# The context stream of a mixture layer in smaller steps, and latent attention with the second mixture on the right side of SBUF

## The chip, the core and the metric

The kernel runs on one core of one Trainium2 chip, as one launch. The metric is the device time of that launch in microseconds (us), the median of several executions.

## What is computed

Two blocks run one after the other on 512 tokens of width 1024, in float32. The first has two layers (attention, then a mixture of 32 experts of which each token takes two); the second has two layers of three mixers and a feed-forward part, on the 512 "latent" tokens and beside them on 256 "context" tokens. The reference, cut:

```python
def first_block(...):
    for i in range(2):
        y = swa_sink_gqa(h, ...) if i == 0 else mla(h, ...)
        h = layer_norm(alpha * h + y, ln_g[i, 0], ln_b[i, 0])
        y = hier_moe(h, ...)               # 4 groups x 8 experts, top 2, hidden 512
        h = layer_norm(alpha * h + y, ln_g[i, 1], ln_b[i, 1])
def hier_moe(...):
    hid = silu(ragged_dot(xs, w_gate, sizes)) * ragged_dot(xs, w_up, sizes)
    ys = ragged_dot(hid, w_down, sizes) * weight
    return segment_sum(ys, tok_sorted)
def second_block(x, c, ctx, c_ctx, ...):
    for layer in range(2):
        u = modulate(rmsnorm(x, ...), sh1, sc1) @ w_in[layer]
        uc = modulate(rmsnorm(xc, ...), sh1c, sc1c) @ w_in[layer]
        # gated linear attention, short convolution, neighbourhood attention
        # (the latent tokens read the context's states, keys and values)
        x = x + g1 * (concatenate([gla_lat, sc_lat, na_lat]) @ w_out[layer])
        x = x + g2 * conv_ffn(modulate(rmsnorm(x, ...), sh2, sc2), ...)
        if layer == 0:                     # the same for the context
            xc = xc + g1c * (... @ w_out[layer]); xc = xc + g2c * conv_ffn(...)
    return rmsnorm(x, final_norm_g)
```

The context's path needs nothing of the first block, so it can run beside it.

## The kernel before, in words

`whole` runs the stages in this order: attention of layer 0; the first mixture (`moe(0)`); latent attention (`mla`); the second mixture (`moe(1)`); the two latent layers of the second block (`mixer`, `ffn`); the final norm. Beside each mixture runs a piece of the context's path, the "context stream": layer 0's context mixers beside the first, `then` (layer 0's context feed-forward and layer 1's context mixers) beside the second.

A mixture takes the 32 experts in 16 pairs p = 0..15. Per expert, 6.29 MB of weights (gate, up, down; 2 MB each) come on SP's DMA queue (line 863) into wide buffers `wx` (and some others: `we` early ones, `ws`, and granules `w`). Per pair, tokens are gathered to columns `xg`; TensorE makes gate and up (L806) into PSUM `sc`; ScalarE (L807) and VectorE (L808) make the hidden rows; TensorE turns them (L815), VectorE copies them out as `hT` (L817, once per pair, so its 16 records are a clock of the pairs); TensorE multiplies by the down weights (L825), ScalarE scales into `y` (L827), and POOL adds the rows into `acc` in HBM with an indirect DMA (L742). After each expert of a pair p > 1 the Python loop calls `fill(n)`, which lets the context stream emit until it has emitted n TensorE instructions. That is the order in which the program is written; a scheduler then orders each engine's instructions, with the context stream's DMAs at high priority, and the pools decide which tile takes whose place: a tile waits until all tiles whose place it takes have been released.

The context stream's matmuls (128x256, PSUM banks `a` and `b`) split every float32 operand in a high and a low part and add three products (L240, L241, L242); the weights' parts `wh` (ScalarE, L235) and `wl` (VectorE, L236) are made on the chip. Its weights come on POOL's queue (L187), its small tables on SP's (L181).

SBUF is used as two stacks, left and right. Before the change the main stages lie on the left and the context stream on the right; `mla_down` (the first part of latent attention), with its weights' parts, lies on the right where the first context piece was, and so do buffers of the second mixture's early weights. In the latent mixers, `xT`, `sp` and `lp` lie on the right, the split weights `wh`, `wl` on the left, where the second mixture was.

`combine` ends a mixture: per tile of 128 tokens, x (read back from `acc`, L979) gets a row sum (L997), mean (L305), squares (L306), centring and gain (L307), a Newton reciprocal root (L274 to L289) and the bias (L309). Before the change its scratch and the vectors `ln_g`, `ln_b` (0.5 MB each when spread over the partitions, L976) take wide buffers, and the two vectors are loaded behind the use of the last gate and up weights.

Of the kernel before, what the change touches and what calls it, by code (L numbers as in the profile page):

```python
# [129 lines left out]
class Net:  # L130
    def __init__(self, nc, tc, ins, ctx):
        self.nc, self.tc, self.ins = nc, tc, ins
        self.side, self.banks, self.size = "left", {}, 1024
        self.cst = {}
        self.load_consts(self.pool(ctx, "consts", 1), 0)
        self.ident = self.c("ident")
        self.hp = self.pool(ctx, "hp", 1)
        self.wp = self.pool(ctx, "wp", 3)
        self.dp = self.pool(ctx, "dp", 1, space=bass.MemoryType.DRAM)

    def beside(self):

        b = copy.copy(self)
        b.side, b.cst, b.size = "right", dict(self.cst), 512
        b.banks = {t: (a, 1) for a, ts in (("a", "mm sc tp ua"), ("b", "po ub dn")) for t in ts.split()}
        return b
# [31 lines left out]
    def dma(self, out, src):  # L178

        with self.tc.high_priority() if self.side == "right" else nullcontext():  # L180
            self.nc.sync.dma_start(out, src)  # L181

    def load(self, out, src):

        if self.side == "right":
# [30 lines left out]
    def psum(self, es, **banks):  # L216

        if self.side == "left":
            self.banks = {t: (t, n) for t, n in banks.items()}
        self.pp = self.pool(es, "pp", 2, space=PSUM)  # L220
# [275 lines left out]
    def mla(self, xt):  # L496

        with ExitStack() as es:
            self.psum(es)
            self.held = ExitStack()  # L500
            self.wides = self.pool(self.held, "wide", 4), 4
            cp = self.pool(es, "cT", 1, "right")
            self.load_consts(cp, 4)
            cT = [cp.tile([128, 5, 512], F32R, name=f"cT{a}") for a in "hl"]
            kr = cp.tile([128, 4, 32], F32, name="kr")
            with self.stage(whp=4, side="right"):
                self.mla_down(xt, cT, kr)
# [105 lines left out]
    def moe(self, i, lg, meanwhile):  # L613
# [9 lines left out]
        with ExitStack() as ep:  # L623
            self.psum(ep, **(dict(mm=1, tp=1) if i else {}))
            self.load_consts(self.php, 3)
            parts = self._moe(i, lg, meanwhile)
        return self.combine(es, *parts)

    def _moe(self, i, lg, meanwhile):
# [205 lines left out]
        def stream(shape):  # L835
# [6 lines left out]
            if n < gen or (i == 0 and 17 <= n < 24):  # L842
                return [self.pool(es, f"early{n}", 1, side="right").tile(shape, F32, name="we")], nullcontext if n >= gen else self.late if n >= first else self.hold[1]
            turn = (n - gen if i or n < 17 else n - gen - 7) + base
# [103 lines left out]
        for p in range(16):  # L948
# [10 lines left out]
            for j in range(2):  # L959
                at, weight = to[2 * p + j]  # L960
                add_rows(at, down(hT[:, :, 64 * j:64 * j + 64], ws[j][2], weight))
                if p > 1:
                    fill(70 if i == 0 else 72)
            if p == 1 or (p == 0 and i == 0):
# [3 lines left out]
            elif p % 4 == 3 and p < 15:  # L968
                to = targets_of(2 * p + 2, 2 * p + 10)
        loaded, added = self.after("SP"), self.after("Pool")  # L970
        finished(beside)
        xs, lnp = self.new_x(), self.wide([128, 2, 1024])
        with loaded():
            lnp = [lnp[:, a] for a in range(2)]
            for w, nm in zip(lnp, ("ln_g", "ln_b")):
                nc.sync.dma_start(w, bcast_rows(ins[nm][i, 1], 1024))  # L976
        for t, x in enumerate(xs):
            with added():
                nc.gpsimd.dma_start(x, self.acc[i][128 * t:128 * t + 128])  # L979
            added = self.after("Pool")  # L980
        return xs, lnp

# [3 lines left out]

    def combine(self, es, xs, lnp):

        nc, V = self.nc, self.nc.vector
        with es:  # L990
# [189 lines left out]
    def mixing(self, l, st, xs=None, src=None, dst=None):  # L1180
# [12 lines left out]
        with ExitStack() as e1:  # L1193
            self.sp = self.pool(e1, "sp", 2, side="right")
            self.load_columns(self.sp, l)
            if not lat:
                self.mixer_pools(e1, l, lat)
            with ExitStack() as e2:
                xp = self.pool(e2, "xTp", 1, side="right")
                self.lp = self.pool(e2, "lp", 2, side="right")  # L1200
                if lat:
# [538 lines left out]
    def ffn(self, l, st, xs=None, rows=None):  # L1740
# [12 lines left out]
        xp = self.pool(e1, "xTp", 1, side="right")  # L1753
        self.sp = self.pool(e1, "sp", 2, side="right")
        self.load_columns(self.sp, l)
        self.lp = self.pool(e1, "lp", 2, side="right")
        tiles = []
# [104 lines left out]
    def whole(self, out):  # L1862
# [23 lines left out]
        xs = list(self.moe(0, lg, lambda: b.mixing(0, 1, src=ins["ctx_2"][0], dst=xc)))  # L1886
        lg = self.mla(xs)
        xs = self.moe(1, lg, then)
        with ExitStack() as es:
            self.psum(es, mm=2, sc=2, tp=2, po=2)  # L1890
            self.banks.update(ua=("mm", 2), ub=("sc", 2), dn=("po", 2))
            for l in range(2):
                xs = finished(self.ffn(l, 0, self.mixer(l, 0, xs)))
            self.sp = self.pool(es, "sp", 2, side="right")
            lp = self.pool(es, "lp", 2, side="right")
            g = lp.tile([128, 1024], F32, name="fg", bufs=1)
# [28 lines left out]
```

## Time and profile before

| | us |
|---|---|
| median of 3 runs | 3430.08 |
| the runs | 3419.17, 3430.11, 3430.08 |
| the profiled execution, whole | 3424.68 |
| its span, first to last instruction | 3422.9 |
| TensorE busy in the span | 3139.3 (92%) |
| first mixture's last `y` (L827) | ends at 920.5 |
| second mixture's first and last `hT` copy | 1256.6 and 1953.4 |

All rows below are of the profiled execution, and their times are microseconds from the start of its span. A median of a few runs lies some us from one execution, here 5.4 us above it.

### The profile page before, as it was taken

How to read it: one execution, taken by the hardware profiler on the slowest of the kernel's cores; microseconds unless marked ns; L12 is line 12 of the kernel's file. 1: busy time of each engine (PE TensorE's matmuls, PEld its weight loads, DVE VectorE, ACT ScalarE, POOL GpSimd, SP SyncE). 2: the span in 40 equal slices, each digit the busy share in tenths (PEclk: the TensorE clock that was granted, in tenths of full speed). 3: DMA queues.
4: the chain of work that ended last, by engine and by line, in shares of the span. 5: the costliest groups of instructions: out<-in, count | busy, mean ns of one | idle time of the engine just before them, and what ended most of it. 6: DMA issues, size and time to landing. Idle time of an engine off the chain costs nothing. (4 is left out here: it accounts for less than half of the span.)

```text
span 3422.9 us, 46600 instructions
## 1 busy us (share of the span) xinstructions
PE 3139.3 (92%) x17508; PEld 2123.4 (62%) x17508; DVE 1655.5 (48%) x4015; ACT 1172.2 (34%) x2322; POOL 406.2 (12%) x538
## 2 busy tenths in 40 slices
PE   8997999999699969999889759999999999999998
PEld 5454445544286636666445257767888777678887
DVE  3454242223266645555423056565555556755555
ACT  3331222222255324333122044344342442543332
POOL 0000221212100013232121100130000000400000
PEclk9998999999899979999999979999999999999999
DMA  8779989999931469888898932223233232333331
GB/s 287 264 272 351 352 327 338 364 355 388 329 121 43 165 225 379 317 321 314 302 359 322 387 99 80 76 74 111 87 99 98 81 92 67 81 100 93 97 94 56
DMA packets 282686, 716.01 MB, mean 209 GB/s; under 512 B 34936, under 2 KB 164008, under 8 KB 234584
## 3 DMA queue, kind: packets, MB, share of 16 engines
q1 hardware_dynamic: 250008, 634.80, 51.4%
q0 software_dynamic: 32448, 78.18, 7.4%
q8 instruction: 140, 2.29, 0.3%
q14 instruction: 90, 0.74, 0.1%
HBM read 691.76 MB, written 37.87 MB: 213 GB/s over the span
## 5 line engine op out<-in xcount | busy, mean ns | idle before, releaser
L236 DVE TENSOR_TENSOR wl<-w,wh 128x1024 fp32r<-128x1024 f32 (+4 forms) x467 | 437.1, 950 | 276.9 <-ACT wh L235 271.9
L235 ACT CAST wh<-w 128x1024 fp32r<-128x1024 f32 (+4 forms) x467 | 377.5, 827 | 512.5 <-PE po L242 116.2
L806 PE MATMUL sc<-wx,xg 128*64 128x512 f32 x1416 | 473.0, 613 | 23.1 <-DMA wx<-in_moe_w_up 16.9
L240 PE MATMUL mm<-xTh,wh 128*128 128x512 f32 (+1 forms) x672 | 263.3, 392 | 11.6 <-ACT xTh L235 6.1
L806 PEld LDWEIGHTS sc<-wx,xg 128*64 128x64 f32 x1416 | 133.0, 139 | 222.4 <-issue 176.9
L242 PE MATMUL mm<-xTh,wl 128*128 128x512 f32 (+1 forms) x672 | 262.2, 390 | 0.9 <-DVE wl L236 0.9
L241 PE MATMUL mm<-xTl,wh 128*128 128x512 f32 (+1 forms) x672 | 260.0, 387 | 0.0
L808 DVE TENSOR_TENSOR hid<-hid,sc 64x512 f32<-64x512 f32 x64 | 43.8, 685 | 304.7 <-ACT hid L807 304.4
L825 PE MATMUL mm<-wx,hT 128*64 128x512 f32 x704 | 173.7, 625 | 10.5 <-DVE hT L817 5.5
L807 ACT ACTIVATE hid<-sc 64x512 f32<-64x512 f32 x64 | 37.8, 591 | 382.5 <-PE sc L806 382.3
L806 PE MATMUL sc<-w,xg 128*64 128x512 f32 x352 | 168.0, 610 | 0.0
L742 POOL DMA_INDIRECT acc<-y,to x64 | 106.9, 1671 | 462.9 <-ACT y L827 262.1
L240 PEld LDWEIGHTS mm<-xTh,wh 128*128 128x128 f32 x672 | 127.9, 190 | 43.0 <-ACT xTh L235 6.6
L241 PE MATMUL sc<-xTl,wh 128*128 128x512 f32 (+1 forms) x384 | 146.0, 380 | 0.0
L242 PEld LDWEIGHTS mm<-xTh,wl 128*128 128x128 f32 x672 | 127.8, 190 | 28.8 <-DVE wl L236 1.3
L240 PE MATMUL sc<-xTh,wh 128*128 128x512 f32 (+1 forms) x384 | 145.6, 379 | 0.0
L242 PE MATMUL sc<-xTh,wl 128*128 128x512 f32 (+1 forms) x384 | 145.1, 378 | 0.0
L241 PEld LDWEIGHTS mm<-xTl,wh 128*128 128x128 f32 x672 | 127.7, 190 | 26.9 <-issue 0.7
L240 PE MATMUL a<-xTh,wh 128*128 128x256 f32 (+2 forms) x472 | 139.6, 296 | 4.7 <-ACT rs L1449 0.9
L240 PE MATMUL po<-wh,gTh 128*128 128x512 f32 x352 | 137.9, 392 | 3.8 <-DVE t2k L1771 2.8
L241 PE MATMUL po<-wl,gTh 128*128 128x512 f32 x352 | 137.1, 390 | 0.0
L242 PE MATMUL po<-wh,gTl 128*128 128x512 f32 x352 | 136.3, 390 | 0.0
(518 smaller groups left out, 6702.7 us busy)
## 6 DMA issues: line engine op xcount, KB each, us to landing
wx<-in_moe_w_up SPq DMA_DIRECT2D x89, 1024.0 KB
wx<-in_moe_w_down SPq DMA_DIRECT2D x88, 1024.0 KB
wx<-in_moe_w_gate SPq DMA_DIRECT2D x88, 1024.0 KB
g<-in_w_ada SPq DMA_DIRECT2D x48, 1024.0 KB
w<-in_ffn_w_up SPq DMA_DIRECT2D x176, 256.0 KB
w<-in_moe_w_gate SPq DMA_DIRECT2D x60, 512.0 KB
w<-in_ffn_w_up POOLq DMA_DIRECT2D x88, 256.0 KB
w<-in_ffn_w_down SPq DMA_DIRECT2D x44, 512.0 KB
```

The lines of the kernel that those rows point to most:

```text
L235: self.nc.scalar.copy(hi, src)
L236: self.nc.vector.tensor_tensor(lo, src, hi.bitcast(F32), op=ALU.subtract)
L240: mm(ps, ah, bh, start=start, stop=False)
L241: mm(ps, ah, bl, start=False, stop=False)
L242: mm(ps, al, bh, start=False, stop=stop)
L742: nc.gpsimd.indirect_dma_start(out=acc, out_offset=bass.IndirectOffsetOnAxis(ap=ix, axis=0), in_=y, in_offset=None, bounds_check=1023, oob ...
L806: nc.tensor.matmul(ps[r], xg[:, k], w, start=k == 0, stop=k == 7)
L807: nc.scalar.activation(hid[own], ps[other], AF.Silu)
L808: V.tensor_tensor(hid[own], hid[own], ps[own], op=ALU.mult)
L825: nc.tensor.matmul(py[64 * h:64 * h + 64], hT[:, k], w[:, 512 * h:512 * h + 512], start=k == 0, stop=k == 3)
```

## The change

The tests `side == "right"` become fields of their own (`second` for the context stream, `far` for the other side). A copy `m` of the main program with the sides swapped runs latent attention and the second mixture on the right; the context stream of the second mixture goes to the left. The latent layers keep their sides, so their left tiles now take the place of the context stream and their right tiles that of the second mixture. `combine` runs after the mixture's own pools are closed, in two small pools of its own, and loads `ln_g` and `ln_b` itself. In the second mixture `fill(72)` becomes `fill(62)`; what the stream has not emitted after the 28 calls is written behind the last expert (`finished(beside)`), ahead of the read-back of `acc`.

```diff
     def beside(self):
         b = copy.copy(self)
-        b.side, b.cst, b.size = "right", dict(self.cst), 512
+        b.side, b.second, b.cst, b.size = "right", True, dict(self.cst), 512
...
-            cp = self.pool(es, "cT", 1, "right")
+            cp = self.pool(es, "cT", 1, self.far)
...
-            with self.stage(whp=4, side="right"):
+            with self.stage(whp=4, side=self.far):
                 self.mla_down(xt, cT, kr)
...
-            parts = self._moe(i, lg, meanwhile)
-        return self.combine(es, *parts)
+            xs = self._moe(i, lg, meanwhile)
+        es.close()
+        return self.combine(i, xs)
...
                 if p > 1:
-                    fill(70 if i == 0 else 72)
+                    fill(70 if i == 0 else 62)
...
-        loaded, added = self.after("SP"), self.after("Pool")
+        added = self.after("Pool")
         finished(beside)
-        xs, lnp = self.new_x(), self.wide([128, 2, 1024])
-        with loaded():
-            lnp = [lnp[:, a] for a in range(2)]
-            for w, nm in zip(lnp, ("ln_g", "ln_b")):
-                nc.sync.dma_start(w, bcast_rows(ins[nm][i, 1], 1024))
+        xs = self.new_x()
...
-    def combine(self, es, xs, lnp):
+    def combine(self, i, xs):
...
+        with ExitStack() as es:
+            cp = self.pool(es, "comb", 2)
+            self.sp = self.pool(es, "csp", 2)
+            lnp = cp.tile([128, 2, 1024], F32, name="lnp", bufs=1)
+            for a, nm in enumerate(("ln_g", "ln_b")):
+                nc.sync.dma_start(lnp[:, a], bcast_rows(self.ins[nm][i, 1], 1024))
...
-                both = self.wide([128, 2, 1024])
+                both = cp.tile([128, 2, 1024], F32, name="lntt")
...
         xs = list(self.moe(0, lg, lambda: b.mixing(0, 1, src=ins["ctx_2"][0], dst=xc)))
-        lg = self.mla(xs)
-        xs = self.moe(1, lg, then)
+        m = copy.copy(self)
+        m.side, m.far = "right", "left"
+        lg = m.mla(xs)
+        b.side = b.far = "left"
+        xs = m.moe(1, lg, then)
```

The names of `combine` have new line numbers in the changed kernel: L976 is L992, L997 is L1000, the mixture's L806 to L828 are one higher, and L1128, L1155 are L1131, L1158.

**Between the first mixture and latent attention, ScalarE.** `wh` are the parts of `mla_down`'s weights, `xTh` the high parts of its turned input (two per tile of 128 tokens), L997 or L1000, and L306, are `combine`'s. Before:

```order
L235 CAST wh_7561<-w_7559 128x768
L827 ACTIVATE y_7349<-mm_7340,wy_6901 128x512
...
L306 ACTIVATE wx_7377,ln_s_7381<-x_7368,ln_n_7380 128x1024
...
L306 ACTIVATE wx_7400,ln_s_7404<-x_7368,ln_n_7403 128x1024
L997 ACTIVATE wx_7446,sums_7447<-x_7368 128x1024
L235 CAST xTh_7498<-tp_7500 128x4x128
L235 CAST xTh_7498<-tp_7507 128x4x128
L306 ACTIVATE wx_7423,ln_s_7427<-x_7368,ln_n_7426 128x1024
L235 CAST xTh_7498<-tp_7514 128x4x128
L235 CAST xTh_7498<-tp_7521 128x4x128
L306 ACTIVATE wx_7446,ln_s_7450<-x_7368,ln_n_7449 128x1024
```

And in the changed kernel:

```order
L828 ACTIVATE y_7363<-mm_7354,wy_6901 128x512
L235 CAST wh_7569<-w_7567 128x768
...
L306 ACTIVATE lntt_7386,ln_s_7390<-x_7368,ln_n_7389 128x1024
L1000 ACTIVATE lntt_7409,sums_7410<-x_7368 128x1024
L235 CAST wh_7587<-w_7585 128x768
L1000 ACTIVATE lntt_7432,sums_7433<-x_7368 128x1024
L306 ACTIVATE lntt_7409,ln_s_7413<-x_7368,ln_n_7412 128x1024
L1000 ACTIVATE lntt_7455,sums_7456<-x_7368 128x1024
L306 ACTIVATE lntt_7432,ln_s_7436<-x_7368,ln_n_7435 128x1024
L306 ACTIVATE lntt_7455,ln_s_7459<-x_7368,ln_n_7458 128x1024
L235 CAST xTh_7506<-tp_7508 128x4x128
L235 CAST xTh_7506<-tp_7515 128x4x128
```

The first `xTh` moved behind the squares (L306) of all four tiles, where it stood behind those of two; on VectorE the low parts `xTl` moved behind L307 and L309 of all four tiles in the same way. The `wh` moved behind the last `y`.

**Between the second mixture and the latent layers, ScalarE.** Here `wh` are the parts of the latent layer's `w_in`, L1128 (L1131) scales a tile by its root. Before:

```order
L827 ACTIVATE y_17111<-mm_17102,wy_16117 128x512
L827 ACTIVATE y_17125<-mm_17116,wy_16117 128x512
L997 ACTIVATE wx_17157,sums_17158<-x_17130 128x1024
...
L235 CAST xTh_17153<-t2k_17235 128x4x128
L1155 ACTIVATE t2k_17272,ss_17274<-x_17130 128x512
L235 CAST xTh_17153<-t2k_17242 128x4x128
L235 CAST wh_17475<-w_17473 128x768
L235 CAST wh_17481<-w_17479 128x768
L235 CAST wh_17487<-w_17485 128x768
L235 CAST wh_17493<-w_17491 128x768
L1128 ACTIVATE t2k_17272<-x_17130,rs_y_17281 128x512
```

In the changed kernel:

```order
L808 ACTIVATE hid_17064<-sc_17065 64x512
L235 CAST wh_17491<-w_17489 128x768
L808 ACTIVATE hid_17064<-sc_17084 64x512
L828 ACTIVATE y_17119<-mm_17110,wy_16094 128x512
L235 CAST wh_17497<-w_17495 128x768
L828 ACTIVATE y_17133<-mm_17124,wy_16094 128x512
L235 CAST wh_17503<-w_17501 128x768
L235 CAST wh_17509<-w_17507 128x768
L1000 ACTIVATE lntt_17176,sums_17177<-x_17138 128x1024
...
L235 CAST xTh_17163<-t2k_17261 128x4x128
L1131 ACTIVATE t2k_17291<-x_17138,rs_y_17300 128x512
```

All four `wh` moved from behind the first tile's `xTh` to the mixture's last expert. VectorE's four `wl` moved with them.

**The same place, SP's queue.** `wx`, `ws` (`in_moe_w_down`) are the last expert's weights, `w<-in_w_in_2` the latent layer's. Before:

```order
L863 DMA ws_17054<-in_moe_w_down 128x2048
L189 DMA w_17479<-in_w_in_2 128x2x384
L189 DMA w_17485<-in_w_in_2 128x2x384
L976 DMA wx_17131<-in_ln_g 128x1024
L976 DMA wx_17131<-in_ln_b 128x1024
```

In the changed kernel:

```order
L864 DMA ws_17062<-in_moe_w_down 128x2048
L189 DMA w_17495<-in_w_in_2 128x2x384
...
L181 DMA pcol_17155<-cols_76 128x320
...
L189 DMA w_17637<-in_w_in_2 128x2x416
L189 DMA w_17643<-in_w_in_2 128x2x416
L189 DMA w_17649<-in_w_in_2 128x2x416
L992 DMA lnp_17173<-in_ln_g 128x1024
L992 DMA lnp_17173<-in_ln_b 128x1024
```

`ln_g` and `ln_b` moved behind five small tables and three more weights, each of which waits until VectorE has split the granule that it takes; their own place is free only when the last down matmul of the mixture has run.

In the second mixture the scheduler keeps the context's matmuls inside: ahead of the gate and up matmuls of pair 1 stood 54 of them and now stand 16, ahead of pair 2 214 and 137, ahead of pair 6 1176 and 1100, ahead of pair 7 1432 and 1369, ahead of pair 9 1611 and 1603, and all 1959 stand ahead of pair 14 in both kernels; none stands behind the last expert. On SP, of four loads of expert weights that stood behind some twenty small tables of the context (pair 8), three stand ahead of them now.

## Rows read from the trace of the kernel before

**Rows 1.** Part 1 of the page: busy time and share of the span, TensorE.

```profile
PE 3139.3 (92%) x17508; PEld 2123.4 (62%) x17508; DVE 1655.5 (48%) x4015; ACT 1172.2 (34%) x2322; POOL 406.2 (12%) x538
```

**Rows 2.** Windows: us, busy of PE PEld DVE ACT POOL, clock, DMA share, GB/s.

```profile
1300.00:1400.00 100.00, 100.00 (x607) 63.38 (x607) 47.78 (x95) 35.74 (x68) 32.11 (x39) 1.00 0.97 362
...
1600.00:1700.00 100.00, 91.65 (x579) 53.40 (x577) 46.24 (x106) 22.49 (x43) 17.66 (x18) 0.96 0.81 286
1700.00:1800.00 100.00, 86.47 (x405) 40.14 (x402) 26.46 (x63) 25.09 (x53) 22.28 (x25) 0.92 0.97 366
1800.00:1900.00 100.00, 93.49 (x568) 48.10 (x567) 32.54 (x83) 26.93 (x47) 12.66 (x13) 0.98 0.90 339
```

**Rows 3.** The second mixture's copies of `hT` (L817), one per pair.

```profile
L817 DVE COPY hT<-tp x16: 655/692/693, 1256.6 to 1953.4; 128x512 f32<-128x512 f32 x16
```

**Rows 4.** Timeline of VectorE: the copies of pairs 8 and 12.

```profile
1674.37 0.66 DVE L817 COPY hT<-tp 128x512 f32<-128x512 f32 x1
...
1857.61 0.69 DVE L817 COPY hT<-tp 128x512 f32<-128x512 f32 x1 [3.29 <-PE tp L815]
```

**Rows 5.** Timeline of TensorE in the second mixture: two context matmuls, one after the other.

```profile
1403.34 0.28 PE L240 MATMUL b<-xTh,wh 128*128 128x256 f32 x1
1403.46 0.28 PE L241 MATMUL b<-xTl,wh 128*128 128x256 f32 x1
```

**Rows 6.** Windows at pair 8 and at the second mixture's end.

```profile
1680.00:1700.00 20.00, 13.62 (x70) 4.90 (x69) 4.08 (x13) 1.91 (x3) 5.69 (x4) 0.89 0.79 266
...
1900.00:1960.00 60.00, 49.15 (x207) 17.50 (x205) 4.82 (x7) 5.60 (x9) 5.80 (x4) 0.97 1.01 409
1960.00:1980.00 20.00, 2.29 (x12) 0.55 (x8) 5.24 (x13) 7.08 (x13) 4.16 (x6) 0.63 0.57 179
1980.00:2000.00 20.00, 7.66 (x26) 6.86 (x27) 17.57 (x59) 13.25 (x28) 0.00 (x0) 0.51 0.40 144
```

**Rows 7.** Timeline of SP's queue at pair 8: issues of small tables and of weights.

```profile
1672.73 1.32 SPq L181 DMA_DIRECT2D mrow<-mod  x2
...
1685.51 0.35 SPq L181 DMA_DIRECT2D xc<-xctx  x1
1685.95 0.41 SPq L863 DMA_DIRECT2D wx<-in_moe_w_gate  x1
...
1687.61 0.67 SPq L863 DMA_DIRECT2D ws<-in_moe_w_up  x1
```

**Rows 8.** Timeline between the first mixture and latent attention.

```profile
919.84 0.69 ACT L827 ACTIVATE y<-mm,wy 128x512 f32<-128x512 f32 x1
...
934.29 0.15 DVE L305 TENSOR_SCALAR ln_n<-sums 128x1 f32<-128x1 f32 x1 [8.03 <-ACT wx L997]
...
938.43 0.15 DVE L305 TENSOR_SCALAR ln_n<-sums 128x1 f32<-128x1 f32 x1
...
938.66 1.94 PE L253 MATMUL tp<-cst,x 128*128 128x128 f32 x8 [19.18 <-DVE ln_n L305]
...
940.80 1.05 ACT L235 CAST xTh<-tp 128x512 fp32r<-128x512 f32 x2
...
972.32 0.90 PE L545 MATMUL tp<-cst,cn 128*128 128x128 f32 x3 [3.35 <-ACT cn L539]
```

**Rows 9.** Timeline between the second mixture and the latent layers.

```profile
1962.39 0.69 ACT L827 ACTIVATE y<-mm,wy 128x512 f32<-128x512 f32 x1 [3.80 <-PE mm L825]
...
1974.31 1.28 DVE L307 SCALAR_TENSOR_TENSOR wx<-x,ln_n,wx 128x1024 f32<-128x1024 f32 x1 [0.31 <-DVE ln_n L305]
...
1986.67 1.97 PE L1124 MATMUL tp<-cst,t2k 128*128 128x128 f32 x8 [24.38 <-ACT t2k L1128]
...
1992.31 2.31 ACT L235 CAST wh<-w 128x768 fp32r<-128x768 f32 x3
...
1993.20 0.69 PE L240 MATMUL mm<-wh,xTh 128*128 128x384 f32 x1 [4.56 <-ACT wh L235]
...
1998.94 0.72 ACT L1128 ACTIVATE t2k<-x,rs_y 128x512 f32<-128x512 f32 x1
```

More of the change, by code (lines that the diff above doesn't have):

```diff
@@ L132, in __init__ @@
         self.nc, self.tc, self.ins = nc, tc, ins
-        self.side, self.banks, self.size = "left", {}, 1024
+        self.side, self.far, self.second, self.banks, self.size = "left", "right", False, {}, 1024
         self.cst = {}
@@ L178, in dma @@
     def dma(self, out, src):
-        with self.tc.high_priority() if self.side == "right" else nullcontext():
+        with self.tc.high_priority() if self.second else nullcontext():
             self.nc.sync.dma_start(out, src)
     def load(self, out, src):
-        if self.side == "right":
+        if self.second:
             with self.tc.high_priority():
@@ L216, in psum @@
     def psum(self, es, **banks):
-        if self.side == "left":
+        if not self.second:
             self.banks = {t: (t, n) for t, n in banks.items()}
@@ L842, in stream @@
             if n < gen or (i == 0 and 17 <= n < 24):
-                return [self.pool(es, f"early{n}", 1, side="right").tile(shape, F32, name="we")], nullcontext if n >= gen else self.late if n >= first else self.hold[1]
+                return [self.pool(es, f"early{n}", 1, side=self.far).tile(shape, F32, name="we")], nullcontext if n >= gen else self.late if n >= first else self.hold[1]
             turn = (n - gen if i or n < 17 else n - gen - 7) + base
@@ L980, in _moe @@
             added = self.after("Pool")
-        return xs, lnp
+        return xs
     def wide(self, shape):
         return self.wides[0].tile(shape, F32, name="wx", tag="wx", bufs=self.wides[1])
-    def combine(self, es, xs, lnp):
-        nc, V = self.nc, self.nc.vector
-        with es:
+    def combine(self, i, xs):
+        nc = self.nc
+        with ExitStack() as es:
[4 more added lines that the diff above has]
+                nc.sync.dma_start(lnp[:, a], bcast_rows(self.ins[nm][i, 1], 1024))
+            lnp = [lnp[:, a] for a in range(2)]
             turn = nullcontext
             for t, x in enumerate(xs):
-                both = self.wide([128, 2, 1024])
+                both = cp.tile([128, 2, 1024], F32, name="lntt")
                 ta, tb = both[:, 0], both[:, 1]
@@ L1193, in mixing @@
         with ExitStack() as e1:
-            self.sp = self.pool(e1, "sp", 2, side="right")
+            self.sp = self.pool(e1, "sp", 2, side=self.far)
             self.load_columns(self.sp, l)
@@ L1198, in mixing @@
             with ExitStack() as e2:
-                xp = self.pool(e2, "xTp", 1, side="right")
-                self.lp = self.pool(e2, "lp", 2, side="right")
+                xp = self.pool(e2, "xTp", 1, side=self.far)
+                self.lp = self.pool(e2, "lp", 2, side=self.far)
                 if lat:
@@ L1752, in ffn @@
             xs = self.rows_in(es, rows)
-        xp = self.pool(e1, "xTp", 1, side="right")
-        self.sp = self.pool(e1, "sp", 2, side="right")
+        xp = self.pool(e1, "xTp", 1, side=self.far)
+        self.sp = self.pool(e1, "sp", 2, side=self.far)
         self.load_columns(self.sp, l)
-        self.lp = self.pool(e1, "lp", 2, side="right")
+        self.lp = self.pool(e1, "lp", 2, side=self.far)
         tiles = []
@@ L1893, in whole @@
                 xs = finished(self.ffn(l, 0, self.mixer(l, 0, xs)))
-            self.sp = self.pool(es, "sp", 2, side="right")
-            lp = self.pool(es, "lp", 2, side="right")
+            self.sp = self.pool(es, "sp", 2, side=self.far)
+            lp = self.pool(es, "lp", 2, side=self.far)
             g = lp.tile([128, 1024], F32, name="fg", bufs=1)
```

## The prediction

> **What bounds the kernel now.** The page comes first: TensorE is busy 92% of the span [rows 1], so on the whole the kernel goes at TensorE's pace, and only the places where it idles, or works at half clock, have much to give. The windows show where they are. In the second mixture TensorE is full at 1300 to 1400 us, and falls to 91.65, 86.47 and 93.49 us per 100 in the three windows from 1600, while the DMA share is 0.97 again from 1700 [rows 2]. The copies of `hT` time the pairs: 15 steps from 1256.6 to 1953.4 us [rows 3], with pair 8 at 1674.37 and pair 12 at 1857.61 [rows 4]. So the eight steps to pair 8 take 417.8 us, 52 each, and are TensorE's; the four to pair 12 take 183.2, 46 each, and are of both; the three to the last take 95.8, 31.9 each. These last are the DMA's: two experts are 12.58 MB, at the 409 GB/s of that window 30.8 us, with the engines' share at 1.01 [rows 6]. Behind the mixture TensorE then does 9.95 us of work in 40, at granted clocks of 0.63 and 0.51 [rows 6]. A smaller hole of the same kind lies at the first mixture's end: 19.18 us [rows 8]. The change touches these three places; everything after some 2040 us is the latent layers, whose order of instructions is the same in both kernels.
>
> **The change part by part.**
>
> *The context's smaller steps.* What moves is only the place of context matmuls among those of the experts. Counted from the two orders, 77 fewer stand ahead of pair 2, 76 ahead of pair 6, 63 ahead of pair 7, 8 ahead of pair 9, and none from pair 14 on. Two follow each other at 0.12 us [rows 5], so TensorE comes to a pair's gate and up matmuls up to 77 x 0.12 = 9.2 us earlier in the stretch that is TensorE's, and nothing of it is left in TensorE's own work by pair 9. The gain, if any, is what the DMA makes of it: wide buffers come free up to 9 us earlier, and the weights of later pairs are fetched earlier. It has idle share to use (0.81 in the window from 1600 [rows 2]). All of it kept would be 9 us; if the DMA gives it back where context work bunches at pairs 8 to 10, it is 0. I take 4, the middle, because the share is 0.97 from 1700 on, where a lead is spent on the one resource that has none over. The order has no context work behind the last expert, so the 31.9 us steps of the tail have no less to carry and no more.
>
> *SP's queue at pair 8.* Issues of small tables run from 1672.73 to 1685.51 us, and four loads of 1 MB follow behind them, the first at 1685.95 and the last at 1687.61 [rows 7]. In the 20 us after 1680 TensorE is busy 13.62 and the DMA share is 0.79 [rows 6]: the queue, not the bytes, was late there. Three of the four now stand ahead of the tables. The idle DMA time in that window is 0.21 x 20 = 4.2 us, which bounds the gain; but these loads also wait for buffers that the preceding pair's down matmuls hold, which a better place does not release. And the context's read-back now stands behind weights that wait, which may hold its next block. From 4 gained to 6 lost (TensorE's 6.38 us idle there, once more); I take 2 gained.
>
> *`combine` in its own pools, first mixture.* Squares and centring of all four tiles now come before the first `xTh` and `xTl`. A tile's period is 938.43 - 934.29 = 4.14 us [rows 8], so the last tile's squares lie 3 periods after the first's, at about 934.3 + 12.4 + 1.3 (the centring takes 1.28 [rows 9]) = 948 us, and `xTh` follows at some 948 to 949, against 940.80 [rows 8]. That is 8 us late. It is not all lost: before, the turned input of tiles 1 to 3 came one period after another, and TensorE's matmuls followed at that pace, with a wait of 3.35 us at 972.32 for the normalised rows [rows 8]; now all four tiles are there at once. I take 5 lost. The ends: nothing lost, if the later tiles catch up wholly; 10, if the low parts on VectorE come one more half period late. The vectors `ln_g`, `ln_b` are now loaded when the last down matmul has run, about 919.8 [rows 8]; the centring that needs them begins at 934.5 (behind the mean at 934.29), and each is a transfer of 0.5 MB. At the 179 GB/s of the other boundary [rows 6] the 1 MB takes 5.9 us; that is hidden under the read-back of `acc`, with some 9 us over.
>
> *`combine` and the sides, second mixture.* Four `wh` and their `wl` now lie on free space of the left and are made during the last expert. Before, the first matmul waited 4.56 us, ended by a `wh`, and went at 1993.20; `wh` x3 took 2.31 us from 1992.31, just ahead of it [rows 9]. Without them it is `xTh` that ends the wait, some 1 to 2 us sooner. The next tile's scaling, at 1998.94, stood behind the fourth `wh` and goes up to 2.7 us earlier, but its turning stands in TensorE's order behind 24 matmuls at half clock. From 5 gained to 0; 2 to 3 is where the `wh` row puts it.
>
> The late vectors work against it. They wait for the last down matmul, at about 1962.4 (the last `y` begins there), and stand behind three weight loads that wait for splits (three `wh` take 2.31 us [rows 9], and the `wl` follow them); so they reach the DMA at some 1966, and the centring wants them at 1974.31 [rows 9]. At the 179 GB/s of that window [rows 6] 1 MB takes 5.9 us: 1972, 2 us in hand, with the read-back of `acc` and the weights in the same engines. The cover is the read-back; if it is gone, the centring waits up to 3 us, and with it the whole chain to 1986.67. I take 0.5 lost, so 2 gained for the place.
>
> The sum: -4 - 2 + 5 - 2 = -3 us. Against the profiled execution, 3424.7, that is 3421.7. The median of the runs shown lies 5.4 us higher than that execution and the lowest run 5.5 below it; I give 3424, half way back to the median.
>
> **The clock, and a rule weighed.** With TensorE idle 24.38 us [rows 9] the granted clock is 0.63 and 0.51, near the lower of its two levels (1.2 of 2.4 GHz) [rows 6]; the 7.66 us of work from 1980 on would be about 4 at full clock. Nothing in the new order fills that hole.
>
> Where the change could hurt is the DMA behind pair 8. At 409 GB/s with the engines' share at 1.01 [rows 6] an expert load of 1 MB is worth 2.6 us. Three context matmuls (the high and low products) use one new weight block of 128x256 floats, 131 KB, or half of one where both token tiles share it; so the 55 matmuls that now bunch between pairs 7 and 9 stand for 9 to 18 blocks, 1.2 to 2.4 MB, 3 to 6 us of DMA time that the expert loads there wait for at most. The sum takes these bytes as moved, not added, and so at nothing. The Trainium skill, "DMA: Bandwidth & Descriptors", section "Queues, rings and completion order", says that each DMA engine takes turns between the queues that have work for it, packet by packet. By that rule a context load on POOL's queue takes half of every engine from the expert load that it meets, whatever SP's order is, and the moved bytes do hurt where the experts are short: the sum would be 0 to +3 instead of -3. No row before shows the two queues' rates apart in one such moment; the rule is the slower rival's second half below.
>
> **The rivals.**
>
> *Faster: the middle of the mixture opens.* From pair 8 to pair 12 the four steps take 183.2 us, while the DMA alone would need 4 x 30.8 = 123 for the experts. What is over, 60 us, is context weights, TensorE's context work and the two waiting on each other: TensorE idles 8.35 + 13.53 + 6.51 = 28.4 us in the three windows from 1600 [rows 2]. If the smaller steps and the new place of the loads let the two overlap, up to 20 of these 28 us come back. For it: DMA share 0.81 in the first of these windows, so bytes could have come earlier. Against it: 0.97 in the second, and context work that ends at the same pair. It would give 3421.7 - 18 = about 3404, at most 3400.
>
> *Slower: the chains at the boundaries grow and nothing comes back.* The place is the first mixture's end. If `xTl` as well as `xTh` waits for all of VectorE's four tiles, the first matmul goes at 952, and the late start passes on undiminished: 11 us; it decides against the change as soon as it exceeds 8, the gains of the other terms. With the gains of the steps at 0 too, the sum is +11 - 2 = +9, about 3434 from the profiled execution, and 3439 from the median. A full slowdown beyond 0.5% needs the bunched context work as well (55 matmuls more from pair 7 to pair 9 than before, 6.6 us of TensorE, and 3 to 6 us of DMA), just where both are short, so that buffers of the tail come free late: +7, and 3446 with the rest.
>
> *It doesn't do what it says.* The rest of the stream behind the mixture is none, by the order of the instructions; the step of 62 or 72 then decides only some 9 us of order, and what remains are the two boundaries: 5 - 2 = +3, 3428 from the profiled execution and 3433 from the median.
>
> **How the numbers follow.** My forecast of small terms that nearly cancel, with the rival in which nothing is done, both within half a per cent of 3430 (17 us, about what a measurement of this kernel can tell from no change): 0.36 and 0.2. The open middle: 0.27, and nearly all of it ends below 3413. The growing chains: 0.17, most of it ending above 3447 only if the bunching is added, which I give about two thirds. With some spill from each case: faster 0.27, same 0.58, slower 0.15. The range goes from 3402, the open middle nearly whole, to 3444, the grown chains from the median; the likeliest case's own is 3412 to 3435.
>
> **What would show it.** Steps: the copies of `hT` up to pair 7 some 5 to 9 us earlier relative to pair 0, and the last one 3 to 6. SP at pair 8: the DMA share above 0.9 in the 20 us where it was 0.79. First boundary: first `xTh` about 28 us behind the last `y` (21 before), and the wait before L545 shorter. Second: no wait for `wh`, first matmul 29 us behind the last `y` (30.8 before). Wrong would be: context matmuls in the hole behind the mixture, a wait of the centring for `ln_g`, or steps between pairs 8 and 12 that sum to under 165 us or over 190.

## The result, and the profile after

The changed kernel takes 3448.02 us in the median of 4 runs (3443.27 to 3449.49); the kernel before, run beside it, 3427.03 (3419.17 to 3430.11). The ratio is 1.0067, with a 95% interval from 1.0052 to 1.0083: some 23 us slower, outside the range that was given. The profiled execution of the changed kernel took 3443.27 us, 18.6 more than that of before.

TensorE runs the same 17508 matmuls and is busy 5.5 us longer (part 1 of the page of the profile; [rows 1] before):

```profile
PE 3144.8 (91%) x17508; PEld 2129.2 (62%) x17508; DVE 1657.9 (48%) x4015; ACT 1172.8 (34%) x2322; POOL 406.4 (12%) x538
```

So most of the loss is in waits; the longer busy time has to do with a stretch at half clock in the latent layers, which comes up below. The pairs of the second mixture, by the copies of `hT` ([rows 3] before), say in which stages the loss arises:

```profile
L818 DVE COPY hT<-tp x16: 682/691/692, 1265.5 to 1964.7; 128x512 f32<-128x512 f32 x16
```

Pair 0 comes 8.9 us later than before and pair 15 11.3 later, though the first mixture's last `y` (L828) comes 2.3 us earlier. Most of the loss is there ahead of the second mixture. The timeline of the first boundary ([rows 8] before) shows it:

```profile
917.59 0.69 ACT L828 ACTIVATE y<-mm,wy 128x512 f32<-128x512 f32 x1 [2.75 <-PE mm L826]
917.95 0.46 SPq L992 DMA_DIRECT2D lnp<-in_ln_g  x1
...
928.01 2.21 POOL L976 DMA_DIRECT2D x<-acc  x4 [5.29 <-issue]
...
931.95 1.06 ACT L1000 ACTIVATE lntt<-x 128x1024 f32<-128x1024 f32 x1 [2.79 <-issue]
...
933.13 0.15 DVE L305 TENSOR_SCALAR ln_n<-sums 128x1 f32<-128x1 f32 x1 [2.78 <-ACT lntt L1000]
...
934.47 1.04 ACT L1000 ACTIVATE lntt<-x 128x1024 f32<-128x1024 f32 x1
...
937.49 1.94 PE L253 MATMUL tp<-cst,x 128*128 128x128 f32 x8 [19.99 <-DVE ln_n L305]
...
942.58 1.06 ACT L1000 ACTIVATE lntt<-x 128x1024 f32<-128x1024 f32 x1 [2.87 <-issue]
...
947.57 0.15 DVE L305 TENSOR_SCALAR ln_n<-sums 128x1 f32<-128x1 f32 x1
...
950.55 1.28 DVE L309 SCALAR_TENSOR_TENSOR x<-lntt,rs_y,lnp 128x1024 f32<-128x1024 f32 x1
...
951.99 1.07 ACT L235 CAST xTh<-tp 128x512 fp32r<-128x512 f32 x2 [2.94 <-issue]
...
952.63 0.69 PE L240 MATMUL mm<-wh,xTh 128*128 128x384 f32 x1 [13.20 <-ACT xTh L235]
```

The first turning (L253) comes 19.9 us behind the last `y`, one later than before (18.8). Its result lies ready in PSUM at 939.4. But `xTh` is written at 951.99, 0.16 us after the last tile's bias (L309) has ended at 951.83, and TensorE waits 13.20 us for it. In between ScalarE is not busy with it: it idles 2.94 us just ahead. The reading is that `xTh` waits for its place: latent attention's first tiles now lie on the left, over `combine`'s two small pools, and these are free when the last tile is done. The experiments test it.

`combine` as a whole ends hardly later than before. In the trace of before its last bias is this one:

```profile
952.18 1.28 DVE L309 SCALAR_TENSOR_TENSOR x<-wx,rs_y 128x1024 f32<-128x1024 f32 x1
```

That is 32.3 us behind the last `y`, against 33.0 in the changed kernel. But there the first `xTh` was written 11 us ahead of it, at 940.80 [rows 8].

The second boundary ([rows 9] before):

```profile
1977.52 0.42 SPq L992 DMA_DIRECT2D lnp<-in_ln_g  x1
1978.00 0.42 SPq L992 DMA_DIRECT2D lnp<-in_ln_b  x1
1979.83 0.59 POOL L976 DMA_DIRECT2D x<-acc  x1 [3.53 <-DMA acc<-y,to]
...
1986.97 1.06 ACT L1000 ACTIVATE lntt<-x 128x1024 f32<-128x1024 f32 x1 [11.07 <-issue]
...
2001.04 1.97 PE L1127 MATMUL tp<-cst,t2k 128*128 128x128 f32 x8 [27.37 <-ACT t2k L1131]
...
2005.99 0.69 PE L240 MATMUL mm<-wh,xTh 128*128 128x384 f32 x1 [2.98 <-ACT xTh L235]
```

The read-back and the first row sum in the trace of before:

```profile
1968.84 0.59 POOL L979 DMA_DIRECT2D x<-acc  x1 [3.94 <-DMA acc<-y,to]
...
1972.66 1.06 ACT L997 ACTIVATE wx<-x 128x1024 f32<-128x1024 f32 x1 [9.59 <-DMA x<-acc]
```

The `wh` are out of the way: the first matmul waits 2.98 us for `xTh`, where it waited 4.56 for `wh`. But the vectors, and two weights of the latent layer just before them, are issued 2 to 4 us ahead of the read-back of `acc`, and its first tile is summed 7.1 us behind its issue, where it took 3.8. From the last `y` at 1973.77 to the first matmul it is 32.2 us; before, 30.8 [rows 9].

In the windows at pair 8 ([rows 6] before) the hole that was there has moved, not closed:

```profile
1680.00:1700.00 20.00, 19.18 (x119) 10.51 (x118) 10.69 (x28) 2.81 (x5) 3.78 (x4) 1.00 0.93 317
1700.00:1720.00 20.00, 14.74 (x55) 4.62 (x53) 1.88 (x7) 0.59 (x1) 1.51 (x1) 0.83 0.82 301
```

SP's queue ([rows 7] before) shows where it went. Three loads of expert weights now go ahead of the small tables, but the tables themselves go 22 us later, and loads of weights stand behind them again:

```profile
1692.56 0.33 SPq L864 DMA_DIRECT2D wx<-in_moe_w_gate  x1
...
1694.79 0.86 SPq L181 DMA_DIRECT2D mrow<-mod  x2
...
1706.20 0.33 SPq L181 DMA_DIRECT2D mrow<-mod  x1
1706.63 0.37 SPq L864 DMA_DIRECT2D ws<-in_moe_w_up  x1
```

### The profile page after: what moved, and what is told of

Same layout as the page of the kernel before. It is cut to its first block, busy times and chain, and to the rows that moved or that the text cites. A ratio compares the mean times of both kernels' runs of the same rounds, so it can differ in the third digit from the quotient of the medians.

```text
span 3441.4 us, 46595 instructions
## 1 busy us (share of the span) xinstructions
PE 3144.8 (91%) x17508; PEld 2129.2 (62%) x17508; DVE 1657.9 (48%) x4015; ACT 1172.8 (34%) x2322; POOL 406.4 (12%) x538
## 5 line engine op out<-in xcount | busy, mean ns | idle before, releaser
L240 PE MATMUL mm<-xTh,wh 128*128 128x512 f32 (+1 forms) x672 | 262.3, 391 | 11.1 <-ACT xTh L235 5.5
L242 PE MATMUL mm<-xTh,wl 128*128 128x512 f32 (+1 forms) x672 | 261.9, 390 | 1.0 <-DVE wl L236 1.0
L240 PEld LDWEIGHTS mm<-xTh,wh 128*128 128x128 f32 x672 | 127.3, 189 | 42.4 <-ACT wh L235 6.0
L240 PE MATMUL a<-xTh,wh 128*128 128x256 f32 (+2 forms) x472 | 139.8, 297 | 6.3 <-ACT wh L235 1.3
L242 PEld LDWEIGHTS mm<-xTh,wl 128*128 128x128 f32 x672 | 127.3, 189 | 28.9 <-DVE wl L236 1.5
L242 PE MATMUL sc<-xTh,wl 128*128 128x512 f32 (+1 forms) x384 | 144.9, 377 | 0.0
L240 PE MATMUL sc<-xTh,wh 128*128 128x512 f32 (+1 forms) x384 | 144.5, 377 | 0.0
L240 PE MATMUL po<-wh,gTh 128*128 128x512 f32 x352 | 138.0, 392 | 3.8 <-DVE t2k L1774 2.8
L242 PE MATMUL po<-wh,gTl 128*128 128x512 f32 x352 | 136.4, 390 | 0.0
```

The lines of the kernel that those rows point to most:

```text
L240: mm(ps, ah, bh, start=start, stop=False)
L242: mm(ps, al, bh, start=False, stop=stop)
```

## The experiments

Each stage is measured from the start of a mixture's last `y`, so that a late or early start of an execution drops out. The table gives, in us, from one trace of each kernel: the first matmul of latent attention (A), the seventh turning of normalised rows (L545; the six ahead of it come together or in two threes; B), and the last `y` of the second mixture (C), each behind the first mixture's last `y`; and the first matmul of the latent layers behind the second mixture's (D). The last column is the ratio to the kernel before, with its interval.

| kernel | A | B | C | D | ratio |
|---|---|---|---|---|---|
| before, first profile | 21.6 | 45.4 | 1042.5 | 30.8 | 1 |
| before, second | 21.3 | 45.1 | 1041.0 | 30.9 | 1 |
| before, third | 21.0 | 45.0 | 1038.4 | 30.6 | 1 |
| changed, first | 35.0 | 58.9 | 1056.2 | 32.2 | 1.0067 (1.0052 to 1.0083) |
| changed, second | 35.5 | 59.1 | 1059.2 | 33.2 | |
| step 62 alone | 21.0 | 45.5 | 1036.7 | 31.1 | 0.9987 (0.9972 to 1.0002) |
| changed, step 72 | 35.2 | 59.0 | 1054.7 | 31.7 | 1.0066 (1.0051 to 1.0082) |
| combine alone | 25.4 | 56.2 | 1045.4 | 30.4 | 1.0036 (1.0020 to 1.0052) |
| combine alone, 4 scratch | 25.1 | 50.0 | 1049.1 | 30.8 | 1.0028 (1.0012 to 1.0043) |
| the same, no vectors | 22.2 | 46.1 | 1039.1 | 30.1 | 1.0021 (1.0004 to 1.0038) |
| changed, combine on the far side | 20.5 | 50.4 | 1047.6 | 31.6 | 1.0034 (1.0017 to 1.0051) |
| the same, 4 scratch | 19.8 | 49.3 | 1045.6 | 31.1 | 1.0050 (1.0032 to 1.0068) |
| the same, 4 scratch, no vectors | 19.7 | 50.5 | 1049.1 | 30.4 | 1.0024 (1.0009 to 1.0039) |
| changed, old combine behind mixture 1 | 32.4 | 55.1 | 1056.7 | 31.2 | 1.0040 (1.0019 to 1.0062) |

**Combine alone.** The sides and the step of before.

```diff
-        m = copy.copy(self)
-        m.side, m.far = "right", "left"
-        lg = m.mla(xs)
-        b.side = b.far = "left"
-        xs = m.moe(1, lg, then)
+        lg = self.mla(xs)
+        xs = self.moe(1, lg, then)
...
-                    fill(70 if i == 0 else 62)
+                    fill(70 if i == 0 else 72)
```

> Only combine's own pools and its own loads of ln_g and ln_b; sides and the step of 72 as before. Theory of the place (the first xTh of latent attention waits because its tiles lie on the left over combine's tiles, which are free only when the last tile's bias is done): xTh on the right is free of that, so it comes about 21 us behind the first mixture's last y, as before (34 in the changed kernel), and the time is that of before within 6 us. Rival, combine itself (late vectors, scratch in two small pools): xTh 30 us or more behind, time 10 us or more above before.

It measured 3435.72 us (3425.1 to 3446.13, 12 runs), 1.0036: about 12 us above before, where the theory had 6 at most. The first `xTh` comes 24.8 us behind the last `y`, neither 21 nor 30; A is 25.4 and B 56.2. So `combine` costs by itself, which the theory of the place did not hold, and the place is not all. Here the vectors go just ahead of the read-back of `acc` (924.38 and 925.57), not 10 us ahead of it as in the changed kernel.

**Combine's pools on the far side.** In `combine` of the changed kernel:

```diff
-            cp = self.pool(es, "comb", 2)
-            self.sp = self.pool(es, "csp", 2)
+            cp = self.pool(es, "comb", 2, self.far)
+            self.sp = self.pool(es, "csp", 2, self.far)
```

> The changed kernel, with combine's two pools on the other side. Theory of the place: xTh 21 to 23 us behind the last y, the wait of 13.2 us for it gone, time 9 to 14 us below the changed kernel, about 1.003 of before. Rival, combine itself: no change from the changed kernel, 1.0067 of before.

3438.51 us (9 runs), 1.0034, 9.5 us below the changed kernel as forecast, and A at 20.5. The timeline of the first boundary:

```profile
920.69 0.69 ACT L828 ACTIVATE y<-mm,wy 128x512 f32<-128x512 f32 x1 [2.75 <-PE mm L826]
...
940.59 1.05 ACT L235 CAST xTh<-tp 128x512 fp32r<-128x512 f32 x2
...
941.20 0.69 PE L240 MATMUL mm<-wh,xTh 128*128 128x384 f32 x1 [0.80 <-ACT xTh L235]
...
943.18 1.28 DVE L309 SCALAR_TENSOR_TENSOR x<-lntt,rs_y,lnp 128x1024 f32<-128x1024 f32 x1
```

Nothing but the side of two pools was changed, and `xTh` is written ahead of the second tile's bias. The wait of 13.20 us is 0.80. The two vectors moved with the pools, to 36 us ahead of the last `y`, but the old combine below loads them early too and waits all the same. This shows the place.

**The step of 72 in the changed kernel**, one number (`fill(70 if i == 0 else 72)`).

> The changed kernel with the step of 72 again. Theory that the boundaries cost and the step nearly nothing: within 5 us of the changed kernel, 1.005 to 1.008 of before; pair 2 some 5 us later from pair 0 than with 62, and the last y at the same distance. Rival, the smaller step bunches context work where DMA is short (pairs 8 and 12) and costs: 8 us or more below the changed kernel.

3448.77 us (6 runs), 1.0066, as the changed kernel. From pair 0 to pair 2 it takes 77.9 us, where the changed kernel took 79.8 and the kernel before 84.9: the forecast of 5 us more with 72 is a miss. The gain up to pair 2 is not the step's.

The order of TensorE's instructions in the traces says why. Ahead of pair 2's copy of `hT` start 123 of the context's matmuls (those of L240 to L242 into banks `a` and `b`) in the changed kernel, with the step of 62 and of 72, and 201 in the kernel before, again with either step (the next experiment). From 72 to 62 the count moves by 7 at most, ahead of pair 3. It is 201 as well where the sides are swapped and `combine` behind the first mixture lies on the far side or is the old one, and with `combine` alone. So the order that was counted ahead of the prediction is not the smaller step's: it comes only with the swapped sides and the small pools on the left together. Why the scheduler orders so then is open.

**The step of 62 in the kernel before**, one number again.

> The kernel before with only the step 62 in place of 72. Theory that the step is nearly nothing: within 5 us of before. Rival, the smaller step costs by itself: 8 us or more above before, with the loss between pairs 7 and 12.

3422.49 us (12 runs), 0.9987, an interval that holds 1, and the order of before. The step by itself is nothing that can be told.

**The old combine behind the first mixture**, in the changed kernel: wide buffers and early vectors there, the new `combine` behind the second.

```diff
+        if i == 0:
+            return self.combine_wide(es, *xs)
         es.close()
         return self.combine(i, xs)
```

> The changed kernel, with the old combine (wide buffers, vectors loaded early) behind the first mixture alone. Theory of the place: latent attention's first tiles still lie on the left, now over the wide buffers that combine uses, so the first matmul on them still comes 33 us or more behind the last y, and the time is within 5 us of the changed kernel or above it. Rival, combine's own pools and late vectors are what costs at the first mixture: first matmul back to 21 to 22 us behind the last y, 10 us or more below the changed kernel.

A stays at 32.4, close to the 33 that the place forecasts, and C at 1056.7: the first tiles now lie over the wide buffers, and TensorE waits 11.9 us behind its first turning. The last bias and the first `xTh`:

```profile
945.59 1.28 DVE L309 SCALAR_TENSOR_TENSOR x<-wx,rs_y 128x1024 f32<-128x1024 f32 x1
...
946.98 1.07 ACT L235 CAST xTh<-tp 128x512 fp32r<-128x512 f32 x2 [2.90 <-DVE x L309]
```

Here the profile itself names the bias as what ended the wait. `combine` is done 4 us sooner than in the changed kernel (28.8 us behind the last `y` for 33.0), and `xTh` comes as much sooner, behind it again. The time, 3438.75 us (8 runs, 3431.26 to 3453.69), 1.0040, missed the forecast: it is 9 us below the changed kernel, near the rival's number, with an interval that overlaps that of the changed kernel. The single trace and the runs do not quite agree here.

**Four scratch tiles instead of two**, on the far side in the changed kernel, and in the kernel with combine alone.

```diff
-                both = cp.tile([128, 2, 1024], F32, name="lntt")
+                both = cp.tile([128, 2, 1024], F32, name="lntt", bufs=4)
```

> The changed kernel with combine's pools on the other side and four scratch tiles instead of two. Theory that a second part of the loss is the third tile's row sum waiting for the first tile's scratch: the rows of L1000 follow at 4 us a tile as before (5 to 6 in the changed kernel), and the time is 3 to 6 us below the kernel with the pools on the other side alone. Rival, the second part is the late vectors beside the read-back: no difference from that kernel.

> The kernel before with combine in its own pools, four scratch tiles instead of two. If two scratch tiles cost: 4 to 8 us below the run with two, first boundary's normalised rows 4 us earlier. If the late vectors cost: as the run with two tiles, the first row sum still 16 to 17 us behind the last y (13 before).

The first measured 3438.99 us (6 runs), 1.0050, no gain, with an interval that overlaps; the second 3434.35 (12 runs), 1.0028, 1.4 us below the run with two, where 4 to 8 were forecast. The rows of L1000 in that second kernel:

```profile
938.68 1.06 ACT L1000 ACTIVATE lntt<-x 128x1024 f32<-128x1024 f32 x1 [11.14 <-DMA x<-acc]
...
941.20 1.04 ACT L1000 ACTIVATE lntt<-x 128x1024 f32<-128x1024 f32 x1
...
942.24 1.04 ACT L1000 ACTIVATE lntt<-x 128x1024 f32<-128x1024 f32 x1
...
945.43 1.04 ACT L1000 ACTIVATE lntt<-x 128x1024 f32<-128x1024 f32 x1
```

and in the kernel with two, with the vectors and the read-back ahead of them:

```profile
924.38 0.46 SPq L992 DMA_DIRECT2D lnp<-in_ln_g  x1
924.89 0.42 SPq L992 DMA_DIRECT2D lnp<-in_ln_b  x1
...
925.57 2.22 POOL L976 DMA_DIRECT2D x<-acc  x4 [3.74 <-issue]
...
934.63 1.06 ACT L1000 ACTIVATE lntt<-x 128x1024 f32<-128x1024 f32 x1 [11.69 <-DMA x<-acc]
...
937.14 1.04 ACT L1000 ACTIVATE lntt<-x 128x1024 f32<-128x1024 f32 x1
...
938.85 1.28 DVE L309 SCALAR_TENSOR_TENSOR x<-lntt,rs_y,lnp 128x1024 f32<-128x1024 f32 x1
...
940.21 1.06 ACT L1000 ACTIVATE lntt<-x 128x1024 f32<-128x1024 f32 x1 [1.94 <-issue]
...
946.32 1.06 ACT L1000 ACTIVATE lntt<-x 128x1024 f32<-128x1024 f32 x1 [2.87 <-issue]
```

From the first row sum to the fourth it is 6.75 us with four tiles and 11.69 with two: with two, the third tile's row sum waits until the first tile's bias is done (L309, 938.85 to 940.13 in this trace). B falls from 56.2 to 50.0, and the first row sum still comes 16.7 us behind the last `y`, so both things named cost in this stage. That is the scratch, shown in its stage; in the whole time it is within the noise.

**No vectors.** Gain one and bias zero, set by VectorE in place of the two loads; this leaves out the layer norm's own gain and bias.

```diff
-            for a, nm in enumerate(("ln_g", "ln_b")):
-                nc.sync.dma_start(lnp[:, a], bcast_rows(self.ins[nm][i, 1], 1024))
+            nc.vector.memset(lnp[:, 0], 1.0)
+            nc.vector.memset(lnp[:, 1], 0.0)
```

> As the run with four scratch tiles on the other side, with the gain set to one and the bias to zero by VectorE in place of the two loads, so it leaves out the second layer norm's gain and bias. If the loads beside the read-back cost: the first row sum behind each mixture 2 to 4 us earlier (about 13 and 10 us behind the last y), 4 to 7 us in all. If not: within 3 us of that run.

> The kernel before with combine in its own pools, four scratch tiles, and the gain set to one and the bias to zero in place of the two loads (so it leaves out the second layer norm's gain and bias). If the late vectors are what is left of the loss with four scratch tiles: first row sum behind the first mixture 13 us behind the last y (16.7 with the loads), time within 4 us of before. If not: 8 us or more above before, as with the loads.

On the far side: 3433.65 us (12 runs), 1.0024, 5 us less than with the loads, but the intervals overlap, and the first row sum comes 12.3 us behind the last `y`, as with them (12.5). The loads are no cost there, but they were not late there either: that kernel issues them 34.6 us ahead of the last `y`. In the kernel with combine alone: 3430.99 (12 runs), 1.0021, about 5 us above the median of before where 4 were forecast; the first row sum is 13.7 behind `y` (16.7 with the loads, 13.3 before), B is 46.1 and C 1039.1, in the range of before. So in that kernel the loads beside the read-back cost some 3 to 4 us of B, and two tiles and late vectors are undone one after the other: B 56.2, 50.0, 46.1, and 45.4 before. What is left for the pools themselves is about 1 us. The ratio of 1.0021 is still above 1 by its interval, and no stage up to the latent layers shows why; its one profile has a half-clock stretch in them, of the kind that follows.

**Both kernels profiled again.**

> The kernel before, profiled a second time. Its first profile shows no stretch at half clock in the neighbourhood attention of either latent layer; the changed kernel and most experiments show one or two, of some 8 us each. If that is chance in each execution: at least one such stretch in this profile or the next. If it belongs to the change: none in both.

> The kernel before, profiled a third time, as the run ahead of it: a half-clock stretch in one of the two latent layers if it is chance, none if it belongs to the change.

> The changed kernel, profiled a second time. The first boundary as in its first profile: the first matmul of latent attention 35 us behind the last y. The half-clock stretch at the neighbourhood attention elsewhere or absent if it is chance, again in the first latent layer if it belongs to the change.

They took 3426.42, 3416.3 and 3455.66 us, and the first boundary came as forecast (A 35.5). The stages repeat within some 2 us up to pair 7. What does not repeat is a stretch in neighbourhood attention at the lower clock (third number from the end of a line: the granted clock, 1.00 in full). In the changed kernel's first profile, in the first latent layer:

```profile
2220.00:2240.00 20.00, 16.09 (x72) 10.54 (x73) 15.63 (x57) 10.88 (x36) 10.70 (x26) 0.82 0.28 65
2240.00:2260.00 20.00, 20.00 (x96) 13.32 (x95) 10.50 (x44) 6.45 (x24) 8.87 (x12) 0.66 0.20 39
```

and in the second profile of before, in the second layer:

```profile
2920.00:2940.00 20.00, 18.94 (x74) 12.31 (x73) 10.73 (x47) 7.47 (x27) 8.83 (x21) 0.57 0.18 35
```

From the first to the last score matmul (L1504 or its like) the stage takes 70.5 to 71.2 us with such a stretch and 62.7 to 64.6 without. It fell in one of six places in the profiles of before, in three of four in the changed kernel's two, and in ten of eighteen in the experiments'. It is not the change's alone, but whether the change makes it likelier is not settled.

In the latent layers little else differs: from their first matmul to the end, less this stage in both, all fourteen profiles take 1299 to 1306 us. Of the 18.5 us between the spans of the first two profiles, C makes 13.6, D 1.4 and this stage 7.0; the first mixture's earlier end takes 2.2 away and the rest of the latent layers 1.2.

## Why the prediction was wrong

The sum was -4 - 2 + 5 - 2 = -3 us; the traces give +13 to +15 for the first boundary (A and B), and +17 for C on the mean of the profiles (1057.7 for 1040.6), so some 3 more within the second mixture, and +2 for D. Together that is some 19 of the 21 to 23 us.

*The step that failed* is the third term, "`combine` in its own pools, first mixture ... I take 5 lost. The ends: nothing lost ...; 10". It measured 13.5 to 14 (B). It was worked out from the order on ScalarE, where `xTh` stands behind the squares of all four tiles, at 948 to 949 us, 28 to 29 behind the last `y`. The row shows 951.99, 34.4 behind it: `xTh` waits for the release of the place below it, behind the last tile's bias, and the order was only a sign of that. Of the 5 to 6 us between the two, the wait behind the last squares is 2.9. Another 2.0 is the period: it priced a tile at the 4.14 us of the first step, though two scratch tiles in place of wide buffers stretch it (the four means, L305, span 14.4 us and not 12.4; in the kernel before, 13.4). The last 1.1 is a later first mean. The late vectors, which it held to be hidden under the read-back with 9 us over, had that time in hand in the changed kernel (issued at 917.95, ahead of the read-back at 928.01), but not with combine alone. Still the read-back itself goes 10.4 us behind the last `y`, for 8.4 before; what in that is the vectors' is not separated. The other half of the term, that the later tiles catch up since they are all there at once, did not happen: B is as late as A.

The shape of the rival on the slower side was right, first matmul at 952 and the late start passing on nearly undiminished (pair 0 comes 11 to 13 us later behind the last `y`); it gave 11 us for it and a small chance, and asked for bunched context work to pass half a per cent. With some 14 us at the boundary the kernel passed it with only some 3 from the second mixture. No run takes the rates of the two DMA queues apart, so the rule that was weighed beside this rival stays untested.

*The steps.* This term, 4 gained, failed too, in its cause. The copies of pair 2 before, and of pairs 2 and 12 in the changed kernel:

```profile
1341.47 0.68 DVE L817 COPY hT<-tp 128x512 f32<-128x512 f32 x1
...
1345.31 0.69 DVE L818 COPY hT<-tp 128x512 f32<-128x512 f32 x1
...
1868.44 0.69 DVE L818 COPY hT<-tp 128x512 f32<-128x512 f32 x1 [1.50 <-PE tp L816]
```

Up to pair 2 the changed kernel gains 5.1 us (79.8 for 84.9), and gives it back and more between pair 2 and pair 12 (523.1 and 523.6 for 511.6 to 516.1). The forecast read this gain as the step's. With 72 it is there too; with 62 in the kernel before it is not (85.4), and with 62, the sides swapped and `combine` on the far side it is not either (84.9). It goes with the order of TensorE's instructions, and that is not the step's, as counted above. The middle did not open (184.8 and 185.2 us from pair 8 to pair 12, 178.7 to 183.2 before). The DMA share at 1680 rose to 0.93, as forecast, but the tables on SP's queue, and the hole with them, only came some 20 us later; measured from pair 8's copy, which is 9 us later itself, the same 20 us have 0.83. From pair 0 to the last `y` it is 708.3 and 711.2 us in the changed kernel, 703.8 to 705.8 before.

*The second boundary.* The `wh` gave about what was forecast (no wait for them, 1.6 us of 4.56 saved). The loads on SP cost more: the centring doesn't wait for the vectors, but the read-back beside them is longer. In the four traces that issue the vectors 2.3 to 3.3 us ahead of the read-back, with one or two weights just before them, its first tile is summed 5.6 to 8.2 us behind its issue, in the ten others 3.8 to 3.9. How much of it is the vectors' and how much the weights' is not separated here; at the first boundary, with combine alone and four scratch tiles, leaving out the vectors took it from 8.4 to 5.5. The price was named, at up to 3 us, and taken at 0.5.

*It doesn't do what it says* was half right: no context work lies behind the mixture, and the step is within the noise; it hardly moves the order. But the boundaries were not worth the 3 us that it kept for them.

What stays open: with combine's pools on the far side, A is better than before, and the whole is still 1.0034. Its B is 5 us late, C 5 to 9, and its single profile has one of the half-clock stretches in the latent layers. Within its second mixture the loss lies behind pair 12: from there to pair 15 it takes 104.2 us, before 95.8 to 96.7, and 96 of the context's matmuls stand between the copies of pairs 12 and 13, where 37 stood. The other kernels with swapped sides have 52 to 72 there and take 96.3 to 102.2. That more context work in the tail costs there is not shown by an experiment of its own. How the rest divides between chance in the latent layers and the change is not told by one profile each. No version here beats the kernel before by more than its interval; the nearest is the step of 62 alone.

## What to carry to other kernels

When work is moved to the other side of a stack of tiles, ask what lies below its first tiles and when that is released; the order of instructions did not show that price here. Price a chain with fewer scratch buffers at its new period, not at the old one. A load that moves next to a read-back which everything waits for can make that read-back longer (8.4 us for 5.5 here), even if its own reader never waits. And before an order is put down to one edit of several, that edit is worth trying alone: the smaller step, which gave the change its name, moved next to nothing.

## What the runs showed of the hardware

The granted clock fell to 0.50, the lower of its two levels, for 17 us at a time while TensorE had no wait at all. In the changed kernel's first profile:

```profile
2236.50:2253.50 17.00, 17.00 (x67) 11.20 (x66) 8.02 (x36) 5.88 (x21) 6.14 (x10) 0.50 0.23 45
```

Ahead of it stood four waits of 0.8 to 1.1 us each in some 15 us, at the neighbourhood attention. Such a stretch came in some executions and not in others of the same kernel; the second latent layer of before has four waits of 0.4 to 1.2 us at the same instructions and no such stretch in its first profile, and has one in its second. Executions of one kernel spread over 27 us (3410.27 to 3437.28 in 26 runs of before), and on the whole the time goes with the mean granted clock: 3410.27 us at 0.962, 3437.28 at 0.956.
